# One late store of a batched matmul shared between SyncE's and GpSimd's queue

## The chip, the cores and the metric

The kernel runs on one core of one Trainium2 chip. The metric is the device time of one execution in microseconds, as the median of several runs. A core has TensorE (PE), VectorE (DVE), ScalarE (ACT), GpSimd (POOL) and SyncE (SP), and the profile counts 16 DMA engines that move data between the chip's memory and the core's SBUF, whichever of the core's engines issues the transfer.

## The reference

```
b1, b2, m, k, n = 8, 16, 256, 512, 384
x:      (b1, b2, m, k) float32
weight: (b1, b2, k, n) float32
return np.matmul(x, weight).astype(np.float32)
```

There are 128 independent products of 256x512 by 512x384. x is 67.1 MB, the weights are 100.7 MB and the output is 50.3 MB, so 218 MB pass the DMA engines.

## The kernel before

**Tiles.** Four products make a group (G = 4), so there are 32 groups (NG = 32), numbered 0 to 31. A group has 2 MB of x, 3 MB of weights and 1.5 MB of output. In the text x30, w30 and "the store of group 30" are its x load, its weight load and its store. Each of 128 SBUF partitions (the rows of a transfer) holds 8 rows of a group's x and, later, 8 rows of its output. x and the weights have two buffers each (XS, WS), the output has four slots (OS) in one tensor `out_sb`; group n uses slot n mod 4.

**Stages of a group.** DVE casts x to bf16 (L171). PE transposes it through an identity matrix (L224), ACT copies the transposed tile to SBUF (L211). DVE and ACT cast the weights to bf16, 11 of 16 pieces on DVE and 5 on ACT (L184); for the first four and the last two groups DVE casts all of them in eight larger pieces (L200). PE multiplies (L242, and L260 for the last group), ACT copies the product to `out_sb` in four parts (L275). PE, ACT and DVE work on neighbouring groups at the same time.

**What sets the order.** Every engine's program is written out by hand, with semaphores between them. All DMAs are issued by SP (L286 to L310) on one queue. After the first four groups, SP goes round a loop: load x of group n, store group n - 4 (LAG = 4), load the weights of group n. Groups 30 and 31 are written out behind the loop (L298 to L302): x30, the store of group 26, the weights of 30 in two halves, x31, the weights of 31 in two halves. Then come the stores of groups 27 to 31 (L303).

- `load_x` (L108) waits until DVE has cast the buffer's former x (L111).
- `load_w` (L126) waits until DVE (L129) and ACT (L130) have cast the buffer's former weights.
- `store` (L142) waits for the landing of the store two groups earlier (L151) and for ACT's four copies of its group (L152), and issues one DMA of 128 rows (L157). Stores of even and odd groups count on two semaphores, `o_out[0]` and `o_out[1]`; those of groups 28 to 30 on `o_end`, the one of group 31 on `o_fin`.
- `copy_out` (L269) waits, ahead of the first copy of a group, until the store that used its slot has landed (L273). The copy itself is L275.
- At the end SP waits for the stores of groups 28 to 30 (shown at L306), counts on a spare semaphore for a while, and waits for the last store (shown at L309).
- GpSimd (L280) makes the identity matrix at the beginning and nothing else.

Of the kernel before, what the change touches and what calls it, by code (L numbers as in the profile page):

```python
# [12 lines left out]
def kernel(  # L13
# [9 lines left out]
    b1, b2, M, K = x.shape  # L23
    _, _, _, N = weight.shape
# [5 lines left out]
    o_rows = out.rearrange("b1 b2 m n -> (b1 b2 m) n")  # L30
# [10 lines left out]
    G = 4  # L41
    C = P // G
    R = G * M // P
    T = R // 2
    SH, SL = 2, 4
    NG = B // G

    XS, WS, OS = 2, 2, 4
# [3 lines left out]
    LAG = 4  # L52
# [6 lines left out]

    PAD = 12  # L60

    ctx.enter_context(tc.tile_critical(sync_engine=mybir.EngineType.Pool, no_gpsimd_drain=True))  # L62

    def sbuf(name, shape, dtype, n):
        return [
            ctx.enter_context(nc.sbuf_tensor(f"{name}{s}", shape, dtype)) for s in range(n)
        ]
# [6 lines left out]
    def sems(name, n):  # L74
        return [tc.alloc_semaphore(f"{name}{s}") for s in range(n)]
# [9 lines left out]
    out_sb = sbuf("out_sb", [P, OS * R, N], fp32, 1)[0]  # L85
# [6 lines left out]
    id_done, x_cast, w_vcast, w_acast, t_made, t_copied, p_made, o_copied = (  # L92
        sems(name, 1)[0]
        for name in (
            "id_done", "x_cast", "w_vcast", "w_acast",
            "t_made", "t_copied", "p_made", "o_copied",
        )
    )
    x_in, w_in, o_out = sems("x_in", XS), sems("w_in", WS), sems("o_out", 2)
    h_in = sems("h_in", G)  # L100
    o_end = sems("o_end", 1)[0]
    o_fin, spare = sems("o_fin", 1)[0], sems("spare", 1)[0]

    BIAS = 8

    def load_x(e, t, U, s):  # L108
        n = t * U + s
        if not isinstance(n, int) or n >= XS:  # L110
            e.wait_ge(x_cast, n * T + (1 - XS) * T)  # L111
        rows = x_rows[bass.ds(n * (G * M), G * M)]
        if is_full(n):
            src = rows.rearrange("(i p r) k -> p i r k", i=G, p=P)
            dst = x_sb[s % XS][:].rearrange("p (i r) k -> p i r k", i=G)
        else:
            src, dst = rows.rearrange("(p r) k -> p r k", r=R), x_sb[s % XS][:]
        e.dma_start(dst, src).then_inc(x_in[s % XS], 16)  # L118

    def is_short(n):  # L120
        return isinstance(n, int) and (n < LAG or n >= NG - 2)

    def is_full(n):
        return isinstance(n, int) and n == NG - 1

    def load_w(e, t, U, s):  # L126
        n = t * U + s
        if not isinstance(n, int) or n >= WS:
            e.wait_ge(w_vcast, n * CV + (1 - WS) * CV)  # L129
            e.wait_ge(w_acast, n * CA + (1 - WS) * CA)  # L130
        d = SL // SH if is_short(n) else 1
        k = SL * KO // d
        for h in range(d):
            sem = h_in[s % WS * 2 + h] if is_short(n) else w_in[s % WS]
            e.dma_start(  # L135
                w_sb[s % WS][:, h * k : (h + 1) * k, :],
                w_rows[bass.ds(n * (G * K) + h * (G // d * K), G // d * K)].rearrange(
                    "(p k) n -> p k n", k=k
                ),
            ).then_inc(sem, 16)  # L140

    def store(e, t, U, s, pieces=1):  # L142
        n = t * U + s
        dram = o_rows[bass.ds(n * (G * M), G * M)].rearrange("(p r) n -> p r n", r=R)
        if is_full(n):
            dram = o_rows[n * G * M : (n + 1) * G * M].rearrange("(i p r) n -> p i r n", i=G, p=P)
        for q in range(pieces):
            rows = slice(q * R // pieces, (q + 1) * R // pieces)
            last = isinstance(n, int) and n >= NG - OS
            if not last and (not isinstance(n, int) or n >= 2):  # L150
                e.wait_ge(o_out[s % 2], (t * (U // 2) + s // 2) * 16 + 16)  # L151
            e.wait_ge(o_copied, n * T + ((q + 1) * T // pieces + BIAS))  # L152
            src = out_sb[:, bass.ds(slot(t, U, s) * R + q * R // pieces, R // pieces)]
            if is_full(n):
                src = src.rearrange("p (i r) n -> p i r n", i=G)
                rows = slice(0, G)
            e.dma_start(out=dram[:, rows], in_=src).then_inc(  # L157
                o_fin if last and n == NG - 1 else o_end if last else o_out[s % 2], 16
            )

    def slot(t, U, s):
        return (t * U + s) % OS
# [106 lines left out]
    def copy_out(e, t, U, s, q):  # L269
        n = t * U + s  # L270
        if q == 0:
            if not isinstance(n, int) or n >= OS:
                e.wait_ge(o_out[s % 2], (t * (U // 2) + s // 2) * 16 + (16 - OS // 2 * 16 + 16))  # L273
        e.wait_ge(p_made, n * T + (q + 1 + BIAS))
        e.copy(  # L275
            out=out_sb[:, bass.ds(slot(t, U, s) * R + 2 * q, 2), :],
            in_=po[(s * T + q) % PO][:, :, :N],
        ).then_inc(o_copied, 1)

    def on_gpsimd(e):  # L280
        e.memset(identity[:], 0.0).then_inc(id_done, 1)  # L281
        e.wait_ge(id_done, 1)
        make_identity(nc, identity[:], nomemset=True)
        e.drain().then_inc(id_done, 1)

    def on_sync(e):  # L286
        U = 2
        for n in range(LAG):
            load_x(e, 0, NG, n)
            load_w(e, 0, NG, n)  # L290
        rounds = (NG - 2 - LAG) // U
        with e.Fori(0, rounds) as t:
            for s in range(U):
                load_x(e, t, U, LAG + s)
                store(e, t, U, s)
                load_w(e, t, U, LAG + s)

        for n in range(LAG + rounds * U, NG):  # L298
            load_x(e, 0, NG, n)
            if n < NG - 1:  # L300
                store(e, 0, NG, n - LAG)
            load_w(e, 0, NG, n)  # L302
        for n in range(NG - 1 - LAG, NG):  # L303
            store(e, 0, NG, n)
        e.wait_ge(o_end, 16 * (OS - 1))
        with e.Fori(0, 4):  # L306
            e.sem_inc(spare, 1)
        for _ in range(PAD):
            e.sem_inc(spare, 1)  # L309
        e.wait_ge(o_fin, 16)  # L310
# [46 lines left out]
    def on_scalar(e):  # L357
# [8 lines left out]
        def step(t, U, s):  # L366
            short = is_short(t * U + s + 1)
            evacuate(e, t, U, s + 1, range(T - 1))
            for q in range(T):
                copy_out(e, t, U, s, q)  # L370
                if q == 0:
                    evacuate(e, t, U, s + 1, range(T - 1, T))
                if q == 0 and short:
                    e.sem_inc(w_acast, CA)
                if q > 0 and not short:
                    last = CA if q == T - 1 else q
                    cast_w(e, t, U, s + 1, range(CV + q - 1, CV + last), q == 1)
# [11 lines left out]
        for q in range(T):  # L389
            copy_out(e, 0, NG, NG - 1, q)  # L390

    on_gpsimd(nc.gpsimd)
    on_sync(nc.sync)
    on_vector(nc.vector)
    on_tensor(nc.tensor)
# [31 lines left out]
```

## Time and profile before

| | |
|---|---|
| median of 3 runs | 517.71 us (517.47 to 517.81) |
| the profiled execution | 517.57 us |
| its span in the profile | 515.8 us |
| DMA, mean over the span | 423 GB/s, 218.18 MB |
| share of the span busy: PE, DVE, ACT, GpSimd | 62%, 77%, 79%, 0% |

The span is the time from the first to the last instruction that the profiler recorded; the execution's time has 1.8 us more around it. Times inside the span are given in us from its start. In the table by stage each line holds a stretch of the span, its length, the busy time of PE, PE's weight loads, DVE, ACT and GpSimd with the number of instructions, the clock granted to TensorE as a share of full speed, the mean busy share of the 16 DMA engines and the GB/s they moved. In the timeline a line holds start, length, engine, line of the program, operation, output and input, and in square brackets the idle time of the engine before it and what ended it. "Landing" is the time from a DMA's issue until its completion has been counted by all 16 DMA engines.

### The profile page before, as it was taken

To read this page: it belongs to the slowest core of one execution; us is meant where nothing else is said; L and a number is where in the kernel's file an instruction comes from. 1 tells how busy PE (TensorE), PEld (TensorE's weight loads), DVE (VectorE), ACT (ScalarE), POOL (GpSimd) and SP (SyncE) were. 2 spreads that over 40 slices of the span, in tenths; PEclk is the share of its full clock that TensorE was granted. 3 is DMA by queue.
4 is the path that set the end of the run, shared out by engine and by line. 5 is a ranking of instruction groups with operands and counts; after the bars stand their busy time and mean duration, and the time that the engine had idled before them with its cause. 6 is when DMAs were issued, how large, how long until landed. Compare 5 with 4: busy or idle time off the path is not lost.

```text
span 515.8 us, 11659 instructions
## 1 busy us (share of the span) xinstructions
PE 320.0 (62%) x4512; PEld 222.0 (43%) x4512; DVE 397.7 (77%) x462; ACT 409.7 (79%) x387; POOL 0.7 (0%) x6
## 2 busy tenths in 40 slices
PE   2276737567586656675655864767657477656871
PEld 2254425444354443453443543535445354434550
DVE  2788757788777897777977778877789777797960
ACT  1365577798978997987998799889798978997751
POOL 0000000000000000000000000000000000000000
PEclk9698878677866877876888686778667876877697
DMA  8999999999999999999999999999999999999996
GB/s 337 428 423 426 437 430 420 435 431 433 431 424 432 430 439 428 429 426 432 433 436 428 423 434 431 437 429 425 430 431 434 433 429 427 430 435 423 421 429 250
DMA packets 15462, 218.18 MB, mean 423 GB/s; under 512 B 1632, under 2 KB 1632, under 8 KB 2656
## 3 DMA queue, kind: packets, MB, share of 16 engines
q1 hardware_dynamic: 15456, 218.11, 99.3%
q8 instruction: 3, 0.05, 0.0%
q14 instruction: 3, 0.02, 0.0%
HBM read 167.77 MB, written 50.33 MB: 423 GB/s over the span
## 4 chain that ended last, share of the span: by engine, by line
DMA 57%; DVE 29%; issue 9%; PE 1%; DVEq 1%; SPq 1%; ACT 0%; POOLq 0%
DMA w_sb<-in_weight_dram 57%; DVE w_bf L184 20%; DVE x_bf L171 5%; DVE w_bf L200 4%; PE po L260 1%; SPq L135 0%; DVEq L334 0%; SPq L118 0%; DVEq L62 0%; DVEq L180 0%; ACT out_sb L275 0%; SPq L130 0%; DVEq L168 0%; DVEq L194 0%; SPq L422 0%
## 5 line engine op out<-in xcount | busy, mean ns | idle before, releaser
L184 DVE CAST w_bf<-w_sb 32x1536 bf16<-32x1536 f32 x286 | 271.9, 951 | 81.1 <-DMA w_sb<-in_weight_dram 73.0
L242 PE MATMUL po<-w_bf,x_t 128*32 128x384 bf16 x3968 | 201.5, 364 | 33.4 <-DVE w_bf L184 25.4
L224 PE MATMUL pt<-identity,x_bf 128*128 128x128 f32 x512 | 113.5, 409 | 149.1 <-DVE x_bf L171 149.1
L184 ACT CAST w_bf<-w_sb 32x1536 bf16<-32x1536 f32 x130 | 191.0, 1470 | 5.1 <-DMA w_sb<-in_weight_dram 1.9
L224 PEld LDWEIGHTS pt<-identity,x_bf 128*128 128x128 f32 x512 | 101.3, 223 | 161.5 <-issue 161.0
L242 PEld LDWEIGHTS po<-w_bf,x_t 128*32 128x32 bf16 x3968 | 117.7, 107 | 116.3 <-issue 51.5
L275 ACT COPY out_sb<-po 128x768 f32 (+1 forms) x128 | 102.5, 800 | 59.7 <-PE po L242 53.9
L211 ACT COPY x_t<-pt 128x1024 bf16<-128x1024 bf16 x128 | 123.6, 1021 | 20.9 <-PE pt L224 20.3
L171 DVE CAST x_bf<-x_sb 128x1024 bf16<-128x1024 f32 x128 | 80.0, 688 | 12.5 <-DMA x_sb<-in_x_dram 11.7
L200 DVE CAST w_bf<-w_sb 64x1536 bf16<-64x1536 f32 x48 | 45.8, 955 | 8.3 <-DMA w_sb<-in_weight_dram 7.0
L211 ACT ACT_TABLE_LOAD x1 | 1.3, 1283 | 10.8 <-PE pt L224 10.8
L260 PE MATMUL po<-w_bf,x_t 128*128 128x384 bf16 x32 | 5.4, 326 | 2.8 <-DVE w_bf L200 2.8
L260 PEld LDWEIGHTS po<-w_bf,x_t 128*128 128x128 bf16 x32 | 3.1, 98 | 5.1 <-issue 3.1
masks.py:199 POOL TENSOR_SCALAR_AFFINE_SELECT identity<-identity 128x128 f32<-128x128 f32 x1 | 0.3, 294 | 0.2 <-POOL identity L281 0.2
L281 POOL MEMSET identity<- 128x128 f32 x1 | 0.2, 205 | 0.5 <-POOLq L62 0.5
L411 POOL MEMSET const-bfloat16-1.0<- 128x1 bf16 x1 | 0.1, 102 | 0.0
L411 POOL MEMSET const-uint8-127<- 128x1 uint8 x1 | 0.1, 102 | 0.0
L411 POOL MEMSET const-float32-0.0<- 128x1 f32 x1 | 0.1, 99 | 0.2 <-issue 0.2
L411 POOL MEMSET const-float32-1.0<- 128x1 f32 x1 | 0.1, 99 | 0.0
## 6 DMA issues: line engine op xcount, KB each, us to landing
w_sb<-in_weight_dram SPq DMA_DIRECT2D x26, 3072.0 KB, 18.2
x_sb<-in_x_dram SPq DMA_DIRECT2D x32, 2048.0 KB, 22.3
out_dram<-out_sb SPq DMA_DIRECT2D x32, 1536.0 KB, 25.0
w_sb<-in_weight_dram SPq DMA_DIRECT2D x12, 1536.0 KB, 16.7
```

The lines of the kernel that those rows point to most:

```text
L171: e.tensor_copy(out=x_bf[s % BS][:, rows].rearrange("p r (s q c) -> p r s q c", s=S, c=KO), in_=x_sb[s % XS][:, rows].rearrange("p r (q s ...
L184: copy(out=w_bf[(s * G + i) % WBS][h * C : (h + 1) * C], in_=w_sb[s % WS][i * C : (i + 1) * C, h * KO : (h + 1) * KO, :],).then_inc(w_vcas ...
L200: e.tensor_copy(out=w_bf[(n * G + d * SH + a) % WBS][h * p : (h + 1) * p], in_=w_sb[n % WS][a * p : (a + 1) * p, r : r + KO, :],).then_inc ...
L211: e.copy(out=x_t[s % TS][:, 2 * q : 2 * q + 2], in_=pt[(s * T + q) % PT][:].bitcast(bf16),).then_inc(t_copied, 1)
L224: ins = e.transpose(pt[(s * T + q) % PT][:, rr, h, :], words[:, 2 * q + rr, h :: KO // 2], identity[:],)
L242: ins = e.matmul(po[(s * T + q) % PO][mine, rr, :N], x_t[s % TS][:, 2 * q + rr, ko // 2, mine, ko % 2], w_bf[(s * G + i) % WBS][:, ko, :], ...
L260: ins = e.matmul(po[(s * T + q) % PO][:, rr, :N], x_t[s % TS][:, 2 * q + rr, ko // 2, :, ko % 2], w_bf[(s * G + q) % WBS][:, ko, :], start ...
L275: e.copy(out=out_sb[:, bass.ds(slot(t, U, s) * R + 2 * q, 2), :], in_=po[(s * T + q) % PO][:, :, :N],).then_inc(o_copied, 1)
L281: e.memset(identity[:], 0.0).then_inc(id_done, 1)
L411: nc = _bacc.Bacc("TRN2", target_bir_lowering=False, num_devices=1)
```

## The change

The store of group 26 (`SHARED` = 32 - 2 - 4) is split. Each of its 128 rows holds 8 output rows of 1,536 bytes. SP stores the first two (`HR` = 2) of each, and does so behind the weights of group 30 instead of ahead of them: behind the loop, `load_w` now stands ahead of `store`. [...]

```diff
+    SHARED, HR = NG - 2 - LAG, 2
...
+    rest_out = sems("rest_out", 1)[0]
...
             src = out_sb[:, bass.ds(slot(t, U, s) * R + q * R // pieces, R // pieces)]
+            if is_shared(n):
+                rows = slice(0, HR)
+                src = src[:, rows]
...
+    def store_rest(e):
+        n = SHARED
+        e.wait_ge(o_copied, n * T + T + BIAS)
+        e.wait_ge(o_out[(n - 1) % 2], 16 + 16 * ((n + 1) // 2))
+        e.inc_swdge_sem([], [], mode="reset_dge_cursor")
+        dram = o_rows[n * G * M : (n + 1) * G * M].rearrange("(p r) n -> p r n", r=R)
+        a = slot(0, NG, n) * R
+        p = 0
+        for k in (5, 120, 3):
+            e.dma_start(
+                out=dram[p : p + k, HR:],
+                in_=out_sb[p : p + k, a + HR : a + R],
+                max_dma_last_dim=(R - HR) // 2 * N * 4,
+            ).then_inc(rest_out, 16)
+            p += k
+
+    def is_shared(n):
+        return isinstance(n, int) and n == SHARED
...
     def copy_out(e, t, U, s, q):
...
                 e.wait_ge(o_out[s % 2], (t * (U // 2) + s // 2) * 16 + (16 - OS // 2 * 16 + 16))
+            if isinstance(n, int) and is_shared(n - OS):
+                e.wait_ge(rest_out, 16 * 3)
...
     def on_gpsimd(e):
...
         e.drain().then_inc(id_done, 1)
+        store_rest(e)
...
         for n in range(LAG + rounds * U, NG):
             load_x(e, 0, NG, n)
+            load_w(e, 0, NG, n)
             if n < NG - 1:
                 store(e, 0, NG, n - LAG)
-            load_w(e, 0, NG, n)
```

## The prediction, made before the changed kernel ran

> **What bounds the kernel now.** First the page, for the overall limit. Its DMA line gives, in 40 slices of the span, the busy tenths of the core's 16 DMA engines.
>
> ```profile
> span 515.8 us, 11659 instructions
> PE 320.0 (62%) x4512; PEld 222.0 (43%) x4512; DVE 397.7 (77%) x462; ACT 409.7 (79%) x387; POOL 0.7 (0%) x6
> DMA  8999999999999999999999999999999999999996
> out_dram<-out_sb SPq DMA_DIRECT2D x32, 1536.0 KB, 25.0
> w_sb<-in_weight_dram SPq DMA_DIRECT2D x26, 3072.0 KB, 18.2
> ```
>
> All 16 DMA engines are busy from the second slice to the last but one; no compute engine is (ACT 79%, DVE 77%). So bytes on the queue set the time, and only the last slice, 12.9 us, leaves something over. I cut it up with the table by stage; its last two columns are the busy share of the 16 engines and GB/s.
>
> ```profile
> 150.00:200.00 50.00, 33.37 (x485) 22.86 (x481) 41.20 (x49) 44.44 (x42) 0.00 (x0) 0.76 1.00 430
> 506.50:506.75 0.25, 0.00 (x0) 0.00 (x0) 0.00 (x0) 0.00 (x0) 0.00 (x0) 1.00 0.35 147
> 507.00:507.25 0.25, 0.00 (x0) 0.00 (x0) 0.00 (x0) 0.00 (x0) 0.00 (x0) 1.00 0.93 381
> 508.50:510.50 2.00, 0.00 (x0) 0.00 (x0) 0.00 (x0) 0.00 (x0) 0.00 (x0) 0.57 1.03 407
> 511.00:511.50 0.50, 0.00 (x0) 0.00 (x0) 0.00 (x0) 0.00 (x0) 0.00 (x0) 0.50 0.28 111
> 511.50:512.00 0.50, 0.00 (x0) 0.00 (x0) 0.00 (x0) 0.00 (x0) 0.00 (x0) 0.50 0.17 68
> 512.00:512.25 0.25, 0.00 (x0) 0.00 (x0) 0.00 (x0) 0.00 (x0) 0.00 (x0) 0.50 0.09 37
> 512.25:512.50 0.25, 0.00 (x0) 0.00 (x0) 0.00 (x0) 0.00 (x0) 0.00 (x0) 0.50 0.06 25
> 513.00:513.50 0.50, 0.00 (x0) 0.00 (x0) 0.00 (x0) 0.00 (x0) 0.00 (x0) 0.50 0.06 25
> 513.50:514.00 0.50, 0.00 (x0) 0.00 (x0) 0.00 (x0) 0.00 (x0) 0.00 (x0) 0.50 0.07 29
> 514.00:514.50 0.50, 0.00 (x0) 0.00 (x0) 0.00 (x0) 0.00 (x0) 0.00 (x0) 0.50 0.00 0
> ```
>
> In steady work 430 GB/s is 26.9 GB/s for each of 16 engines. The last store runs at 407, 25.4 each. By 511.0 most engines are done. From 512.25 to 514.0 the rate is 25 to 29 GB/s at a busy share of 0.06, a sixteenth: **one DMA engine works alone.** At 512.00 to 512.25 it is 37, one engine for the whole slice and a second for half of it, so the second-latest ends near 512.1. The late one is alone for 514.0 - 512.1 = 1.9 us. The stores of the end show the same engine from the other side, by when they land and when SP (SyncE) stops waiting for them:
>
> ```profile
> 481.23 25.30 SPq L157 DMA_DIRECT2D out_dram<-out_sb  x5
> L157 SPq DMA_DIRECT2D out_dram<-out_sb x1: 391/391/391, 506.1 to 506.1; - x1
> DMA to landing us min/median/max: 8.4/8.4/8.4
> SPq L306 <- DMA out_dram<-out_sb: 3.9, 1, 3.9
> SPq L309 <- DMA out_dram<-out_sb: 1.6, 1, 1.6
> ```
>
> The last store (L157) is issued at 506.1 and lands 8.4 us later, at 514.5. Issuing ends at 481.23 + 25.30 = 506.5, and SP then waits 3.9 us (L306), to 510.4, for the three stores ahead of it, though at 506.5 to 506.75 only 147 of 430 GB/s flow: most engines have nothing left, and a few still carry old stores. So the end is not the compute chain's alone; it is the backlog of one engine, which is the later by 1.9 us.
>
> **The change, part by part.** The store of group 26 is 1,536 KB, 12,288 bytes in each of 128 rows. SP keeps two eighths (3,072 bytes a row); GpSimd sends 9,216 bytes a row in three DMAs of 5, 120 and 3 rows, two runs of 4,608 bytes a row.
>
> (1) *Rows taken off one engine.* Dealt evenly, 128 rows over 16 engines are 8 each, 73,728 bytes of GpSimd's part. 120 rows at 8 each need 15 engines, so one gets none of them; of the parts of 5 and 3 it gets at most one row each. It carries 6 to 8 rows fewer, the others 8 or 9. At 26.9 GB/s a row is 9,216 / 26,900 = 0.34 us; 6 rows are 2.06 us and 8 are 2.74. I take 6, the end that gains less.
> If the engine with the short share is the late one, it ends at 514.0 - 2.06 = 511.9, and the second-latest, at 512.1, sets the end, or at 512.1 + 0.34 = 512.4 where it has a ninth row. The rest of the way to the end is unchanged. So this gains 1.6 to 1.9 us.
>
> Which engine is spared, no view tells. [...]
>
> (2) *The queue of SP.* These rows give the order around the change: w and x loads and stores of groups 29 to 31, and how long two stores (groups 25 and 26), then the weights of group 29 and of group 31, took to land.
>
> ```profile
> 434.16 0.36 SPq L157 DMA_DIRECT2D out_dram<-out_sb  x1
> 448.74 0.33 SPq L135 DMA_DIRECT2D w_sb<-in_weight_dram  x1
> 449.73 0.39 SPq L157 DMA_DIRECT2D out_dram<-out_sb  x1
> 464.46 0.80 SPq L135 DMA_DIRECT2D w_sb<-in_weight_dram  x2
> 465.32 0.42 SPq L118 DMA_DIRECT2D x_sb<-in_x_dram  x1
> ...
> DMA to landing us min/median/max: 25.4/25.4/25.4
> ...
> DMA to landing us min/median/max: 25.8/25.8/25.8
> ...
> DMA to landing us min/median/max: 18.2/18.2/18.2
> ...
> DMA to landing us min/median/max: 11.4/11.4/11.4
> ```
>
> Group 26's store is no longer issued at 449.73 but behind w30 (464.46), so near 465.3, and x31 moves 0.4 us to 465.7. Both enter a queue that is 18 us deep or more, so the issue costs nothing; without that depth it would cost the 0.4 us. SP's waits at this store (group 24's landing, group 26's copies) are long met by then. w30 moves up by the store's 1.57 MB / 430 GB/s = 3.7 us less what GpSimd has sent by then. Nobody waits for it: DVE starts on w30 at 480.32, straight behind earlier casts:
>
> ```profile
> 461.52 2.91 DVE L184 CAST w_bf<-w_sb 32x1536 bf16<-32x1536 f32 x3
> 466.99 7.83 DVE L184 CAST w_bf<-w_sb 32x1536 bf16<-32x1536 f32 x8 [2.55 <-DMA w_sb<-in_weight_dram]
> 480.32 7.86 DVE L200 CAST w_bf<-w_sb 64x1536 bf16<-64x1536 f32 x8
> 488.21 2.50 DVE L171 CAST x_bf<-x_sb 128x1024 bf16<-128x1024 f32 x4
> 491.81 7.86 DVE L200 CAST w_bf<-w_sb 64x1536 bf16<-64x1536 f32 x8 [1.09 <-DMA w_sb<-in_weight_dram]
> 493.11 0.80 ACT L275 COPY out_sb<-po 128x768 f32<-128x768 f32 x1 [0.39 <-PE po L242]
> ```
>
> (3) *GpSimd's waits and DMAs.* Its first wait, for group 25's store, ends at 434.16 + 25.4 = 459.6; behind it stand only the three DMAs and the end of the program. Then 1.18 MB (2.74 us of all engines) compete with w29, which lands at 448.74 + 18.2 = 466.9 and for which DVE has waited 2.55 us. w29 is late by something between 0 (GpSimd's first bytes come after 466.9) and 2.74 us (all of them go ahead of it). I take 0.7, nearer the low end: rows of 24,576 bytes (3,072 KB over 128) stand on SP's side against runs of 4,608, and the late engine, which sets w29's landing, has few of the latter.
> DVE is then busy without a gap from 466.99 to 490.7 and waits 1.09 us for w31 (480.32 + 11.4 = 491.7). With 6 rows fewer on the late engine w31 lands up to 2.06 us sooner, so DVE starts it between 490.8 and 490.7 + 2.74 = 493.4 instead of 491.81. The last store's issue moves with it: between 1.0 sooner and 1.6 us later. Its data reach an idle engine 0.9 us after issue (506.1 to 507.0) and are through by 511.3, 0.8 us ahead of the second-latest engine. A shift of 1.6 us later would end at 512.9, 0.5 to 0.8 us past the new end; at 0.7 for w29 the issue is earlier than before, and it costs nothing.
>
> (4) *The added wait in ACT's copy of group 30.* It needs all three parts landed, and takes place at 493.11. Before, the slot was free at 449.73 + 25.8 = 475.5. From 459.6 there are 33.5 us for 2.74 us of data, so I cost it at nothing; if that cover fails it costs in full, since PE's next product waits for the copy.
>
> (5) *The end of SP's program* (L306 to L309) takes 514.5 - 1.6 - 510.4 = 2.5 us beside the last store. The three stores ahead of it land sooner on the same engine, so it stays hidden behind the last landing.
>
> (6) *Smaller runs.* 3,072-byte runs went at 25.4 GB/s per engine against 26.9, so about 0.007 us per run; 18 runs of 4,608 bytes at that price are 0.13 us. Two queues in turn on one engine are not in this trace: from nothing to, say, the 0.39 us of a DMA's issue in all. I take 0.1 on the second-latest engine.
>
> **Sum.** New end of data: between 512.1 and 512.4, middle 512.2, plus 0.1 is 512.3; 514.0 - 512.3 = 1.7 us gained. The profiled execution took 517.57 us, 1.8 outside its span, 0.14 under the median of 517.71. 517.57 - 1.7 = **515.9 us**.
>
> **The rivals.**
> *A: spared engine is the late one, w29 hardly late* (515.4 to 516.3 us). For it: one engine alone by 1.9 us, against 2.06 us taken off.
> *B: like A, but w29 is late by most of 2.74 us*, and two queues cost more. The last store then sets the end: 0.7 to 1.2 us gained, 516.4 to 516.9. Against it: SP's rows are over five times as long as GpSimd's runs.
> *C: the spared engine is not the late one*, and the change doesn't do what it can do. The late engine has 8 or 9 rows: as before, or 0.34 + 0.13 later; 517.5 to 518.1 us. For it: the table by stage shows one late engine, not which.
> [...]
> [...]
> [...]
>
> **How the numbers follow.** A 0.55, B 0.08, C 0.22, D 0.15. Faster by over 0.2% (1.04 us, about what a measurement of this kernel can tell from no change) is A and half of B: 0.59. Within 0.2%: half of B and C, 0.26. Slower: D, 0.15. The range leaves out D and A's rims: 515.3 to 518.2 us.
>
> **What would show it.** (1) right: the last 2 us of DMA at a sixteenth are gone, and the last store lands in about 7 us or less after an issue near 505.5. C: still one engine alone to the end. (3): DVE's wait before the weights of group 29 grows by 0.7 (A) or 2 to 3 us (B). [...] Wrong altogether would be a lower rate between 460 and 490: two queues then cost throughput on all engines.

## The result and the profile after

The changed kernel takes 516.23 us (median of 11 runs, 515.88 to 516.44) and the kernel before, beside it, 517.50 us (517.39 to 517.96). The ratio is 0.9973, 95% interval 0.9964 to 0.9982: faster by 1.27 us. The prediction gave 515.9 us, or 1.7 us less than its profiled execution. The profiled execution of the changed kernel took 516.31 us, with a span of 514.5 us, 1.3 us shorter than before.

The page first. Compare its last slice with that of before, and look for the new queue.

```profile
span 514.5 us, 11664 instructions
PE 319.1 (62%) x4512; PEld 223.0 (43%) x4512; DVE 397.6 (77%) x462; ACT 409.5 (80%) x387; POOL 3.7 (1%) x9
DMA  8999999999999999999999999999999999999997
q0 software_dynamic: 368, 1.18, 0.6%
```

The bytes and the compute are the same; GpSimd's 1.18 MB now go through a queue of their own (q0), and the last slice is 0.7 busy instead of 0.6. The table by stage shows why. Its last two columns are the busy share of the 16 DMA engines and GB/s.

```profile
506.50:506.75 0.25, 0.00 (x0) 0.00 (x0) 0.00 (x0) 0.00 (x0) 0.00 (x0) 1.00 0.92 381
512.00:512.25 0.25, 0.00 (x0) 0.00 (x0) 0.00 (x0) 0.00 (x0) 0.00 (x0) 0.50 0.06 25
512.25:512.50 0.25, 0.00 (x0) 0.00 (x0) 0.00 (x0) 0.00 (x0) 0.00 (x0) 0.50 0.08 33
512.50:513.00 0.50, 0.00 (x0) 0.00 (x0) 0.00 (x0) 0.00 (x0) 0.00 (x0) 0.50 0.00 0
```

Data end by 512.5, where one engine ran alone to 514.0 before. At 506.50 the engines are still nearly full (381 GB/s instead of 147): the last store now comes in time for most of them. But 25 to 33 GB/s, little more than a sixteenth of 430, is all that moves from 512.0 to 512.5: one engine is still the last, by half a microsecond at most. The last store's own rows, and SP's two waits at the end, say the same:

```profile
481.70 24.12 SPq L163 DMA_DIRECT2D out_dram<-out_sb  x5
L163 SPq DMA_DIRECT2D out_dram<-out_sb x1: 391/391/391, 505.4 to 505.4; - x1
DMA to landing us min/median/max: 7.7/7.7/7.7
SPq L334 <- DMA out_dram<-out_sb: 3.2, 1, 3.2
SPq L337 <- DMA out_dram<-out_sb: 1.6, 1, 1.6
```

The last store is issued at 505.4 (506.1 before) and lands at 513.1 (514.5 before). The three stores ahead of it have landed at 481.70 + 24.12 + 3.2 = 509.0, against 510.4.

The trace also records 16 counts for each landing (1,632 for the 102 DMAs of the kernel before), and when each comes in; they are read here as one from each DMA engine. No view prints them, so here they stand in words. Of the last store's counts, the last came at 514.5 and the one ahead of it at 512.5 in the kernel before; in the changed kernel they come at 513.1 and 512.4. They also show how the kernel before got there: the distance between the last count of a transfer and the one ahead of it was next to nothing around 300 us, 0.5 us around 385 and 1.1 us at 464. So, if the last count is the same engine's throughout, that engine was not held up by one event; it lost ground over the last 200 us.

The timeline shows the moved and added steps: GpSimd's three DMAs, SP's store behind the weights, DVE's casts and ACT's first copy of group 30.

```profile
460.52 3.02 POOL L176 DMA_DIRECT2D out_dram<-out_sb  x3 [458.81 <-DMA out_dram<-out_sb]
461.51 2.91 DVE L209 CAST w_bf<-w_sb 32x1536 bf16<-32x1536 f32 x3
465.37 0.45 SPq L163 DMA_DIRECT2D out_dram<-out_sb  x1
467.47 7.83 DVE L209 CAST w_bf<-w_sb 32x1536 bf16<-32x1536 f32 x8 [3.04 <-PE po L267]
488.69 2.50 DVE L196 CAST x_bf<-x_sb 128x1024 bf16<-128x1024 f32 x4
491.10 7.86 DVE L225 CAST w_bf<-w_sb 64x1536 bf16<-64x1536 f32 x8
494.88 0.80 ACT L302 COPY out_sb<-po 128x768 f32<-128x768 f32 x1 [1.69 <-PE po L267]
```

DVE starts on w29 at 467.47 instead of 466.99. The view puts this wait down to PE, but the product for which the cast waits, that of group 27, was done before 460; w29, issued at 448.76, lands 18.6 us later, at 467.4, so it is w29 that ends the wait. From there DVE works without a pause, and starts on w31 at 491.10 instead of 491.81. ACT's copy waits for PE and for no DMA.

### The profile page after: what moved, and what is told of

It is laid out like the page before. It is cut to its first block, busy times and chain, and to the rows that moved or that the text cites. A ratio compares the mean times of both kernels' runs of the same rounds, so it can differ in the third digit from the quotient of the medians.

```text
span 514.5 us, 11664 instructions
## 1 busy us (share of the span) xinstructions
PE 319.1 (62%) x4512; PEld 223.0 (43%) x4512; DVE 397.6 (77%) x462; ACT 409.5 (80%) x387; POOL 3.7 (1%) x9
## 3 DMA queue, kind: packets, MB, share of 16 engines
q0 software_dynamic: 368, 1.18, 0.6%
## 4 chain that ended last, share of the span: by engine, by line
DMA 52%; DVE 31%; issue 10%; PE 3%; ACT 1%; DVEq 1%; SPq 1%; ACTq 0%; POOLq 0%
DMA w_sb<-in_weight_dram 52%; DVE w_bf L209 20%; DVE x_bf L196 6%; DVE w_bf L225 5%; PE po L267 1%; PE po L285 1%; ACT w_bf L209 1%; ACT out_sb L302 0%; SPq L138 0%; DVEq L362 0%; SPq L121 0%; ACT x_t L236 0%; DVEq L64 0%; DVEq L205 0%; DVEq L193 0%
## 5 line engine op out<-in xcount | busy, mean ns | idle before, releaser
L267 PE MATMUL po<-w_bf,x_t 128*32 128x384 bf16 x3968 | 199.0, 361 | 33.5 <-DVE w_bf L209 21.7
L249 PE MATMUL pt<-identity,x_bf 128*128 128x128 f32 x512 | 115.1, 415 | 151.7 <-DVE x_bf L196 151.7
L249 PEld LDWEIGHTS pt<-identity,x_bf 128*128 128x128 f32 x512 | 103.4, 224 | 163.6 <-issue 163.4
L176 POOL DMA_DIRECT2D out_dram<-out_sb x3 | 3.0, 1010 | 458.8 <-DMA out_dram<-out_sb 458.8
```

What stands on the lines that cost most here:

```text
L176: e.dma_start(out=dram[p : p + k, HR:], in_=out_sb[p : p + k, a + HR : a + R], max_dma_last_dim=(R - HR) // 2 * N * 4,).then_inc(rest_out, 16)
L249: ins = e.transpose(pt[(s * T + q) % PT][:, rr, h, :], words[:, 2 * q + rr, h :: KO // 2], identity[:],)
L267: ins = e.matmul(po[(s * T + q) % PO][mine, rr, :N], x_t[s % TS][:, 2 * q + rr, ko // 2, mine, ko % 2], w_bf[(s * G + i) % WBS][:, ko, :], ...
```

## The experiments

Each run is compared with runs of the kernel before on the same chip; times are medians, with the 95% interval of the ratio. **Theory 1**, the prediction's: the gain is the data that are taken off one late DMA engine. **Theory 2**, the rival: it comes from the new order and from a second queue, whichever engine carries the rows.

**No engine spared.**

```diff
-        for k in (5, 120, 3):
+        for k in (128,):
-                e.wait_ge(rest_out, 16 * 3)
+                e.wait_ge(rest_out, 16 * 1)
```

> The changed kernel with GpSimd's share in one DMA of 128 partitions, eight for every DMA engine, so that no engine is spared. Theory 1 (the gain is the 2.06 us of data taken off the one late DMA engine): the gain is gone, 517.5 us (517.2 to 517.9), and one engine works alone for 1.5 to 2 us at the end. Theory 2 (the gain comes from the order, weights ahead of the store, and from a second queue, whichever engine carries the rows): 516.2 us as the changed kernel.

Measured: 518.14 us against 517.86 (ratio 0.9998 to 1.0016). The gain is gone, as theory 1 said. The table by stage, near the end of this run:

```profile
512.50:513.00 0.50, 0.00 (x0) 0.00 (x0) 0.00 (x0) 0.00 (x0) 0.00 (x0) 0.50 0.09 37
513.50:514.00 0.50, 0.00 (x0) 0.00 (x0) 0.00 (x0) 0.00 (x0) 0.00 (x0) 0.50 0.06 25
514.00:514.50 0.50, 0.00 (x0) 0.00 (x0) 0.00 (x0) 0.00 (x0) 0.00 (x0) 0.50 0.07 29
514.50:515.00 0.50, 0.00 (x0) 0.00 (x0) 0.00 (x0) 0.00 (x0) 0.00 (x0) 0.50 0.00 0
```

One engine alone is back, and it ends up to 0.5 us later than before, though every engine carries the same bytes if the 128 rows are dealt evenly. That points to a cost of GpSimd's DMA itself, but one profiled run is all there is for it: the interval of the medians includes no change.

**Another engine spared.** Parts of 8 and 120, of 120 and 8, and of 4, 120 and 4, with the number in ACT's wait to match. The last:

```diff
-        for k in (5, 120, 3):
+        for k in (4, 120, 4):
```

The expectations call the engine that the parts of 5, 120 and 3 spare "place 5"; the name is the author's, and no run shows the place of an engine. First the parts of 8 and 120:

> [...] If the late engine is at place 5 (theory 1), it has 8 or 9 rows and the gain is gone: 517.5 us (517.2 to 518.0). If sparing any engine helps (theory 2): 516.2. [...]

Measured: 518.39 us against 517.86 (1.0004 to 1.0022). The parts of 120 and 8:

> [...] Theory 1, with the late engine at place 5: 517.5 us (517.2 to 518.0), one engine alone at the end for about 2 us. Theory 2: 516.2 us. [...]

Measured: 518.25 us against 517.86 (1.0000 to 1.0018). The parts of 4, 120 and 4:

> [...] If the late engine is at place 5: no gain and the cost of GpSimd's runs on top, 518.2 us (517.8 to 518.5). If it is not the place that decides: 516.2 us.

Measured: 518.44 us against 517.79 (1.0002 to 1.0021), and the table by stage has one engine at work to the end of the data, later than before:

```profile
514.00:514.50 0.50, 0.00 (x0) 0.00 (x0) 0.00 (x0) 0.00 (x0) 0.00 (x0) 0.50 0.06 25
514.50:515.00 0.50, 0.00 (x0) 0.00 (x0) 0.00 (x0) 0.00 (x0) 0.00 (x0) 0.50 0.04 16
```

All three are slower than the kernel before by 0.4 to 0.65 us and slower than the changed kernel by about 1.7 to 1.9. Theory 2 falls: the same order and the same second queue gain nothing unless the short share falls to the right engine.

The counts of w30's second half, which lands as GpSimd's parts end or later, show that an engine was spared each time, and that it was not the late one. In these three runs one count comes 0.9 to 2.0 us ahead of all others, and the last still comes 1.7 to 1.9 us behind the one ahead of it (1.2 in the kernel before). In the even deal no count comes early, and the last is about 1 us behind. In the changed kernel none comes early and none late: the last is 0.1 us behind.

Which of the 16 engines is the late one, these runs do not name. The parts of 8 and 120 and of 120 and 8 ran on a chip on which no run had the parts of the changed kernel; those of 4, 120 and 4 ran on the same chip as the runs with more and fewer bytes below, which have the parts of 5, 120 and 3 and gain 1.63 and 1.02 us.

**The order alone**, and nothing from GpSimd:

```diff
             load_x(e, 0, NG, n)
+            load_w(e, 0, NG, n)
             if n < NG - 1:
                 store(e, 0, NG, n - LAG)
-            load_w(e, 0, NG, n)
```

> The kernel before with one edit: behind the loop the weights are loaded ahead of the store, and SP still stores all of group 26; GpSimd sends nothing. Theory 1: no engine is spared, so 517.5 us (517.3 to 517.7). Theory 2 as far as it rests on the order alone: 516.2 to 516.8 us.

Measured: 517.77 us against 517.86 (0.9992 to 1.0010): no change.

**The order undone**, with GpSimd's parts kept: the same edit turned round in the changed kernel. It ran twice, the second time beside the changed kernel.

> The changed kernel with SP's two output rows of group 26 again ahead of the weights of group 30. If the gain is the spared engine's alone, 516.2 us (516.0 to 516.5) as the changed kernel; if the order has a part in it beside the split, 516.6 us or more.

Measured: 516.96 us against 517.79 (0.9974 to 0.9992), only 0.83 us gained.

> The changed kernel with SP's two output rows of group 26 ahead of the weights of group 30, once more, beside the changed kernel. If the order has a part in the gain: 0.4 us slower than the changed kernel in the same call, with a landing of group 26's rows while GpSimd's are under way. If the first run of it was a wide spread only: the same as the changed kernel.

> The changed kernel once more, on the same chip as the three runs beside it, so that they can be set against it and not only against the kernel before: 1.27 us under the kernel before, as the first time.

Measured side by side: the changed kernel 516.19 us and the order undone 516.88, against 517.67 (0.9958 to 0.9981 and 0.9981 to 0.9999). So the changed kernel's gain came out again, at 1.48 us, and the order is worth 0.7 us of it by the medians, though alone it is worth nothing. The two intervals just touch, and with the order undone the times spread: 22 runs lie between 516.38 and 518.25, where the 18 of the changed kernel lie between 515.88 and 516.47. The stages from 468 to 476, where GpSimd's data flow, show a loss. First the changed kernel, then the first run with the order undone:

```profile
468.00:472.00 4.00, 2.31 (x55) 1.23 (x44) 3.88 (x5) 3.93 (x5) 0.00 (x0) 1.00 1.03 435
472.00:476.00 4.00, 0.00 (x0) 0.00 (x0) 3.88 (x6) 3.95 (x4) 0.00 (x0) 0.68 1.01 426
```

```profile
468.00:472.00 4.00, 2.26 (x52) 1.19 (x44) 3.88 (x5) 3.93 (x5) 0.00 (x0) 1.00 1.04 407
472.00:476.00 4.00, 0.00 (x0) 0.00 (x0) 3.88 (x6) 3.95 (x4) 0.00 (x0) 0.66 1.01 393
```

The engines are as busy, but move less: 400 GB/s on the mean instead of 430. In the second pair of runs it is 406 (398 and 413) against 422 (417 and 427). Where SP's rows of 3,072 bytes and GpSimd's of 4,608 flow at the same time, both of them stores, 16 to 30 GB/s are lost for some 8 us: 0.3 to 0.6 us at 430 GB/s. With the weights in between, SP's store comes when GpSimd's are nearly through. In the first run's profile DVE then waits 1.15 us for w31 again, the last store is issued at 506.6, and 104 GB/s flow from 512.0 to 512.5, so several engines end late and not one alone; in the second run's the last store is issued at 505.4, as in the changed kernel. That the meeting of the two stores costs the 0.7 us is argued from these rates; no edit tests it by itself.

**More and fewer bytes off the late engine.**

```diff
-    SHARED, HR = NG - 2 - LAG, 2
+    SHARED, HR = NG - 2 - LAG, 1
```

with runs of 5,376 bytes, and the same line with `HR` = 4.

> The changed kernel with HR = 1: SP keeps one output row of eight, GpSimd sends 10,752 bytes a partition in two runs of 5,376, and the spared engine carries 6 x 10,752 = 64.5 KB less instead of 55.3. If the late engine still sets the end of the changed kernel, another 0.34 us are gained: about 515.9 us. If the second-latest engine sets it, as the prediction had it, nothing more is gained: 516.2 us or a little more.

Measured: 516.16 us against 517.79 (0.9950 to 0.9978), 1.63 us gained.

> The changed kernel with HR = 4: GpSimd sends 6,144 bytes a partition in two runs of 3,072, and the spared engine carries 6 x 6,144 = 36.9 KB less instead of 55.3. If the gain goes with the bytes taken off the late engine, 0.69 us of it are lost: about 516.9 us. If two thirds of the relief were enough: 516.2 us.

Measured: 516.77 us against 517.79 (0.9972 to 0.9990), 1.02 us gained.

So 36.9, 55.3 and 64.5 KB taken off gain 1.02, 1.27 (1.48 the second time) and 1.63 us. The gain goes with the bytes, at 0.61 us for 27.6 KB or 0.022 us per KB, where the data rate of an engine would give 0.037 (1 / 26.9). The intervals overlap, so the slope is rough. That fewer bytes gain less is the firmer half of it: the fastest of the 11 runs with `HR` = 4, 516.54 us, is above the slowest of the changed kernel. The version with `HR` = 1 has the lowest ratio of all (0.9964), from 5 runs, but its 516.16 us stand beside 516.23 and 516.19: that it beats the changed kernel is not shown.

**One run per partition instead of two.**

```diff
-                max_dma_last_dim=(R - HR) // 2 * N * 4,
+                max_dma_last_dim=(R - HR) * N * 4,
```

> The changed kernel with GpSimd's bytes of a partition as one run of 9,216 bytes instead of two of 4,608, so 8 or 9 runs on most engines instead of 16 or 18. If each run costs an engine some 0.03 us (the 0.3 us by which the even deal was slower than the kernel before, over 16 runs, is 0.02; the late engine's end says 0.03), 0.1 to 0.25 us are gained over the changed kernel; if the cost lies with the bytes or with the queue, nothing.

> HR = 1 (GpSimd sends 10,752 bytes a partition) as one run of 10,752. If the bytes taken off the late engine still count (theory 1), 0.34 us under the changed kernel in the same call, as the run with HR = 1 and two runs was against the kernel before; with a cost for each run, up to 0.25 us more. If the three engines that end just ahead of the late one set the end, hardly more than 0.4 us in all.

Measured: 518.56 us, and with `HR` = 1 518.62, against 517.67 (1.0006 to 1.0024 and 1.0009 to 1.0027). Both expectations missed by far: the whole gain is gone. The table by stage of the first:

```profile
513.50:514.00 0.50, 0.00 (x0) 0.00 (x0) 0.00 (x0) 0.00 (x0) 0.00 (x0) 0.50 0.06 25
514.00:514.50 0.50, 0.00 (x0) 0.00 (x0) 0.00 (x0) 0.00 (x0) 0.00 (x0) 0.50 0.06 25
514.50:515.00 0.50, 0.00 (x0) 0.00 (x0) 0.00 (x0) 0.00 (x0) 0.00 (x0) 0.50 0.04 16
```

It is the picture of the runs that spare another engine, and the counts of w30's second half bear it out: one comes 2.2 us ahead of all others (2.4 with `HR` = 1), and the last 1.5 us behind the one ahead of it (1.9). By these counts the same three parts are dealt otherwise with one run a partition, and the late engine keeps its share. It is not the number of packets by itself: the profile counts 208 on GpSimd's queue in both runs (368 in the changed kernel), but 208 also with `HR` = 4, where the trace has 6,144 bytes to a packet, both runs of a partition in one, and the gain was kept. Which engine was spared here, the profile doesn't name; why the deal changes is open.

## Why the prediction was right, and where its sizes were off

**(1) Rows taken off one engine: right.** This step carries the change. Four other ways to deal the same bytes gain nothing (128 rows in one part, and the parts of 8 and 120, of 120 and 8, and of 4, 120 and 4), nor does the deal with one run a partition, and the picture of one engine alone goes and comes with the gain. How many rows each engine gets was the author's estimate, and that the spared one carries 6 fewer, and not 7 or 8, no run shows; what the runs showed in its place is one count 0.9 to 2.0 us ahead of all others in the three runs that spared an engine other than the late one.

**The size was too large: 1.7 us forecast, 1.27 measured (1.48 the second time).** Step (1) said that with 2.06 us taken off, the second-latest engine sets the end. It does not: one engine is still alone from 512.0 to 512.5. The last data moved by about 1.5 us (514.0 to 512.5), the last landing by 1.4. So of the 2.06 us the late engine won 1.4 to 1.5. The step also took the rest of the way to the end as unchanged, with the late engine behind by a fixed amount. The counts say otherwise: from w31's second half to the last store the distance of the last count from the one ahead of it grew from 1.2 to 2.0 us in the kernel before, and from 0.1 to 0.7 in the changed one. If it is the same engine, the sparing brought it level, and it then fell behind again. Part of the missing 0.6 us may be the price of GpSimd's runs: dealt evenly, the same bytes end up to 0.5 us later, over 16 runs on the late engine. Step (6) put 18 runs at 0.13 us and two queues in turn at nothing to 0.39, and took 0.1 on the second-latest engine alone. With 4 runs on the late one this price is an eighth of a microsecond, if it goes by runs. Some 0.4 us stays unexplained; in the profile of the changed kernel's second run the last landing came 0.3 us sooner, at 512.8.

**(2) The queue of SP: right alone, wrong beside GpSimd.** The order by itself is worth nothing (517.77 against 517.86), as the step said. That nobody waits for w30 is not the whole of it, though: beside GpSimd's part the move is worth 0.7 us, most likely because it keeps SP's store from flowing at the same time. The prediction had counted bytes and issue times, and not which kinds of transfer share an engine. That the time still came near the forecast is in part luck: with the old order the same reasoning would have forecast the same 1.7 us, and 0.8 was measured.

**(3) GpSimd's DMAs beside w29: right.** 0.7 us late was taken; w29 is late by 0.5 (DVE starts at 467.47 instead of 466.99). The last store is issued 0.7 us sooner, at 505.4 where "near 505.5" was forecast, and DVE's wait for w31 is gone. It lands 7.7 us after its issue, where about 7 or less was given as the sign. Rival B, a w29 late by 2 to 3 us, falls.

**(4) ACT's added wait: right.** The copy waits for PE, and its start at 494.88 is that of the work ahead of it. So D, the slower outcome with its 0.15, did not come. It stood for data of GpSimd too late for this copy, on an estimate of the author's that no run shows; what the trace shows in its place are packets of GpSimd from 464.7 on and their last landing at 478.9, 16 us ahead of the copy. Still, GpSimd's data came late: GpSimd issues from 460.52 to 463.54, and its queue shows no packet before 464.5. From 460 to 464.5, then from 464 to 466:

```profile
q1 hardware_dynamic: 97, 1.88, 97.0%
```

```profile
q0 software_dynamic: 34, 0.04, 5.7%
```

What held them back no run shows. The 4 us cost nothing because the data had over 30 us to land.

**(5) The end of SP's program: right.** SP still waits 1.6 us (L337) for the last store after its other work, so that stays hidden.

**Rival C** did not come true in the changed kernel, but in six of the experiments: sparing the wrong engine, or none, gives 0.3 to 0.95 us more than the kernel before, where the rival had 0 to 0.5.

## What to carry to other kernels

When all DMA engines are busy to the end, look at the last microseconds in fine slices: a rate of a sixteenth (25 to 29 GB/s of 430 in the kernel before) meant that one engine was behind. Moving a whole transfer did not help it here (517.77 us against 517.86); a transfer dealt unevenly did (516.23 against 517.50), but the gain hung on which engine was spared, down to how the bytes of a partition were cut (518.56 with one run instead of two). It was worth 0.7 us more with SP's part of the store behind the weights.

## What the runs showed of the hardware

- One DMA engine of 16 ended some 1.9 us behind the others in the kernel before. By the counts of the last landing it was 2.0 us behind the next there, and 2.0 to 2.9 us in the seven kernels that did not spare it.
- That distance built up slowly: next to nothing around 300 us, 1.1 us at 464 and 2.0 us at the end of the kernel before.
- From 468 to 476, with loads on SP's queue and GpSimd's store on the other, the DMA engines moved 417 to 435 GB/s in two runs of the changed kernel, and 418 and 433 with one queue in the kernel before. They moved 4 to 7% less (393 to 413 GB/s) in the two runs where SP's part of the store flowed at the same time.
- The even deal through GpSimd's queue, with the bytes of every engine unchanged if the 128 rows fall evenly, delayed the last data by up to 0.5 us and the median by 0.3 us, at the rim of what these runs can tell.
- One run of 9,216 bytes a partition instead of two of 4,608 undid the whole gain: 518.56 us against 516.19 beside it.
